# The first and the last pair of gate/up tiles in the FFN of a DiT step: a plain product ahead of the combined operands, and a read-back within the last pair

## The chip, the cores and the metric

The kernel runs on one core of one Trainium2 chip. Its time is the device time of one execution in microseconds (us); lower is better. The engines are called PE (TensorE, matmuls; PEld is its weight load), DVE (VectorE), ACT (ScalarE), POOL (GpSimd) and SP (SyncE, which issues nearly all DMAs here).

## The reference

One denoising step of a network with two layers, the first with differential attention, the second with a Hyena long convolution. Each is followed by a SwiGLU feed-forward network (FFN). The model's width is 1024, that of the FFN 2816. There are 1024 latent tokens and 128 context tokens, 1152 in all. Everything is float32. The part that the change touches is:

```python
def rmsnorm(x, g, eps=EPS):
    y = xf * lax.rsqrt(jnp.mean(xf * xf, axis=-1, keepdims=True) + eps)
    return (y * g.astype(jnp.float32)).astype(x.dtype)

def modulate(h, shift, scale):
    return h * (1.0 + scale) + shift

def swiglu(h, w_gu, w_down):
    g, u = jnp.split(h @ w_gu, 2, axis=-1)
    return (jax.nn.silu(g) * u) @ w_down
...
    for i in range(DEPTH):
        ...
        xs = xs + g1 * out
        h = modulate(rmsnorm(xs, norm2_g[i]), sh2, sc2)
        xs = xs + g2 * swiglu(h, ffn_w_gu[i], ffn_w_down[i])
```

Latent and context tokens have their own shift, scale and gate.

## The kernel before

Activations lie transposed: features on the 128 partitions, tokens along the free axis. `xk[k]` (k = 0 to 7) holds 128 features for all tokens as a left and a right half of 576 tokens. Each fp32 product is three products of parts: a number is split into a high part, copied by ACT (line 1550), and a low part, the difference, by DVE (line 1551), both in `part`; `three` (lines 305 to 307) adds high × high, high × low and low × high in PSUM.

The FFN of a layer (`ffn`) has three stages.

`project` multiplies by the output projection and adds the residual (line 857), in three chunks of 384 tokens. The norm of a chunk is `step(c)`: squares are summed over k on POOL (`nacc`, line 420), PE adds them over the partitions (430), a few tiny instructions on ACT and DVE make the reciprocal root (437 to 444), PE spreads it over the partitions (449), DVE multiplies (889) and ACT applies scale and shift (891). The left half's operands `b0` (k 0 to 3) and `b1` (k 4 to 7) are split in the same step; chunk 2 (tokens 768 to 1151) lies wholly in the right half.

`gate_up` goes through 22 tiles of the FFN's width. Tile t has a gate and an up part, which together form a pair: 2 × 2 blocks (gate and up; k 0 to 3 and k 4 to 7) times 2 × 2 blocks (k halves; left and right tokens). The kernel takes seven products in place of eight, after Winograd: p1, p2, p6, p7, p5, p4, p3, each 4 k × 2 column halves × 3 = 24 matmuls of 128x288, so 168 a pair. Their weight sides come from sums of the four weight blocks, made on POOL (`side_sums`), their token sides are b0, b1, b2 (right half, k 4 to 7) and t1 to t4, differences and sums of blocks of both halves that are formed once per layer by `combos`:

```python
        def second():
            for k in range(4):
                tt(u[:, k], b[k], f(low[0][0], k), SUB)
                tt(u[:, k], u[:, k], f(low[0][1], k), SUB)
                tt(v[:, k], b[k + 4], u[:, k], SUB)
                self.part(t2[0][:, k], t2[1][:, k], v[:, k])
```

`second` makes t2 for p6, `third` t3 for p7, `first` t1 for p5, `fourth` t4 for p4 (on POOL), `last` b2 for p3. The results, silu(gate) × up for each half, go to DRAM as `d_a[l][t]` (lines 1064 and 1072). A `pr` tile is a pair of PSUM banks, three of them in turn. Pairs 0 and 1 are interleaved: p1 and p2 of both come first, while the operands are formed.

`down` reads `d_a` back (line 1131) in groups of tiles, `GROUPS = [2, 4, 4, 4, 4, 4]`, splits them into `hs` tiles (six of them, three a group), multiplies with `mm` tiles of 128x384 in PSUM (six banks) and adds to x, which is loaded again by `load_x` (line 838, from `d_r`). It does so once per group. Weight tiles pass through `raw` (two buffers) to `wh` and `wl` (three each), by `fetch` (line 291).

Within `gate_up` the order on PE, DVE, ACT and POOL is the order in which the code is written (`pin`). A scheduler sets the order on SP, and everywhere else. Every engine works its instructions in order and waits on semaphores.

Of the kernel before, what the change touches and what calls it, by code (L numbers as in the profile page):

```python
# [150 lines left out]
class Net:  # L151
# [720 lines left out]
    def project(self, l, bx):  # L872
# [11 lines left out]

        def step(c):
            rs = self.rstd(c)
            for k in range(KT):
                for x, s, e, _ in self.whole(c, k):
                    nc.vector.tensor_tensor(out=x, in0=rs[:, s:e], in1=x, op=ALU.mult)
                for x, s, e, g in self.x(c, k):  # L890
                    nc.scalar.activation(x, x, AF.Identity, scale=a[:, k, g : g + 1], bias=sh[:, k, g : g + 1])  # L891
# [27 lines left out]

    def combos(self, low, bx, tp):  # L920
        nc, tt = self.nc, self.tt
        ADD, SUB = ALU.add, ALU.subtract
        t1, t2, t3 = (self.operand(tp, f"t{j}") for j in range(1, 4))
        top = self.operand(bx, "b2")
        u, v = (self.tl(tp, [P, 4, HALF], tag="t4" + n) for n in "hl")
        f = lambda t, k: t[:, k].bitcast(F32)
        b = [self.xk[k][1] for k in range(KT)]
        self.ops = ops = {1: low[0], 2: low[1], 3: top, 5: t1, 6: t2, 7: t3}

        def second():  # L930
            for k in range(4):
                tt(u[:, k], b[k], f(low[0][0], k), SUB)
                tt(u[:, k], u[:, k], f(low[0][1], k), SUB)
                tt(v[:, k], b[k + 4], u[:, k], SUB)
                self.part(t2[0][:, k], t2[1][:, k], v[:, k])

        def third():
            for k in range(4):
                tt(b[k], b[k + 4], b[k], SUB)
                self.part(t3[0][:, k], t3[1][:, k], b[k])  # L940

        def first():
            for k in range(4):
                self.part(t1[0][:, k], t1[1][:, k], u[:, k])

        def fourth():
            for k in range(4):
                tt(b[k], f(low[1][0], k), v[:, k], SUB, nc.gpsimd)
                tt(b[k], b[k], f(low[1][1], k), ADD, nc.gpsimd)
            t4 = ops[4] = self.operand(tp, "t4")  # L950
            for k in range(4):
                self.part(t4[0][:, k], t4[1][:, k], b[k])

        def last():
            for k in range(4):
                self.part(top[0][:, k], top[1][:, k], b[k + 4])

        return second, third, first, fourth, last
# [706 lines left out]
```

## Time and profile before

| | us |
|---|---|
| median of three runs | 3252.56 (3246.09 to 3252.89) |
| the profiled execution | 3253.19 |
| its span | 3251.4 |
| PE busy | 3081.2 (95%) |
| DVE busy | 1946.7 (60%) |
| ACT busy | 1183.5 (36%) |
| POOL busy | 1012.0 (31%) |

The mean granted clock of PE is 0.971 of full speed. In a row of instructions the first number is the start in us, the second the duration; "out<-in" are the program's tiles without their buffer numbers; "[1.44 <-DVE xk L857]" says that the engine was idle for 1.44 us just before, and what ended it. An engine's busy time counts overlapping matmuls once. In rows of groups stand count, busy time in us, mean of one in ns, and idle time ahead of them.

### The profile page before, as it was taken

What the parts mean: (1) busy time and instruction counts of PE and PEld (TensorE: products, weight loads), DVE (VectorE), ACT (ScalarE), POOL (GpSimd) and SP (SyncE); (2) the same over time, 40 slices, a digit from 0 to 9 for tenths busy, and PEclk for the clock granted to TensorE, in tenths of its full rate; (3) what the DMA queues carried; (4) which work ended last, traced back from release to release, by engine and by line L of the source; (5) the groups of instructions that cost most, each with busy time, mean ns of one, the idle gap of its engine ahead of it and who ended that gap; (6) DMA issues with size and microseconds to landing.
All of it is one profiled execution on the core that took longest, in us unless ns stands there. A gap on an engine that the chain in (4) does not pass through costs nothing.

```text
span 3251.4 us, 53225 instructions
## 1 busy us (share of the span) xinstructions
PE 3081.2 (95%) x21322; PEld 2988.6 (92%) x21322; DVE 1946.7 (60%) x3139; ACT 1183.5 (36%) x2284; POOL 1012.0 (31%) x866
## 2 busy tenths in 40 slices
PE   7899999999996999998999999999977999998998
PEld 5689989999995999998999999999976999998998
DVE  7866524988637544544544588875456544546555
ACT  3541224888634222222211442335543222222214
POOL 5844301444323434432000313131224434430003
PEclk9999999999996999999999999999987999999999
DMA  6665452444220222224563233345511222225221
GB/s 247 212 203 174 143 159 63 100 96 100 92 93 18 82 75 75 75 74 152 198 221 137 98 118 112 126 164 195 173 45 52 71 78 72 75 74 206 71 80 65
DMA packets 163343, 379.14 MB, mean 117 GB/s; under 512 B 17263, under 2 KB 80119, under 8 KB 160408
## 3 DMA queue, kind: packets, MB, share of 16 engines
q1 hardware_dynamic: 147720, 353.37, 33.0%
q10 hardware_dynamic: 13968, 17.65, 1.5%
q0 software_dynamic: 1408, 4.72, 0.4%
q8 instruction: 168, 2.75, 0.4%
q14 instruction: 79, 0.65, 0.1%
HBM read 278.94 MB, written 96.73 MB: 116 GB/s over the span
## 4 chain that ended last, share of the span: by engine, by line
PE 80%; DVE 6%; DMA 4%; ACT 2%; issue 2%; POOL 1%; SPq 0%; POOLq 0%; ACTq 0%; DVEq 0%
PE mm L305 13%; PE mm L306 13%; PE mm L307 12%; PE pr L306 10%; PE pr L307 10%; PE pr L305 10%; PE tr L785 4%; PE sc L759 2%; PE tr L776 2%; PE sc L760 2%; PE tr L368 1%; PE tr L307 1%; PE tr L305 1%; PE tr L306 1%; ACT xk L891 1%
## 5 line engine op out<-in xcount | busy, mean ns | idle before, releaser
L305 PE MATMUL mm<-hs,wh 128*128 128x384 f32 x1824 | 611.3, 338 | 17.5 <-ACT hs L1550 17.5
L306 PE MATMUL mm<-hs,wh 128*128 128x384 f32 x1824 | 614.2, 337 | 0.4 <-POOL hs L463 0.3
L307 PE MATMUL mm<-hs,wl 128*128 128x384 f32 x1824 | 612.5, 336 | 0.0
L857 DVE SCALAR_TENSOR_TENSOR xk<-mm,ada,xk 128x192 f32<-128x192 f32 (+3 forms) x560 | 233.3, 453 | 335.5 <-PE mm L307 329.8
L1165 DVE TENSOR_TENSOR xk<-pr,xk 128x576 f32<-128x576 f32 x220 | 166.0, 755 | 424.8 <-PE pr L307 228.2
L305 PEld LDWEIGHTS mm<-hs,wh 128*128 128x128 f32 x1824 | 343.5, 189 | 23.1 <-ACT hs L1550 18.0
L306 PEld LDWEIGHTS mm<-hs,wh 128*128 128x128 f32 x1824 | 344.2, 189 | 4.2 <-issue 1.8
L307 PEld LDWEIGHTS mm<-hs,wl 128*128 128x128 f32 x1824 | 344.0, 189 | 2.2 <-issue 0.8
L420 POOL TENSOR_TENSOR nacc<-nacc,nsq 128x384 f32<-128x384 f32 x104 | 119.2, 1146 | 703.1 <-ACT nsq L416 701.2
L1165 POOL TENSOR_TENSOR xk<-xk,xk 128x576 f32<-128x576 f32 x88 | 127.6, 1450 | 568.2 <-DVE xk L1165 454.1
L1550 ACT ACTIVATE wh<-raw 128x1024 fp32r<-128x1024 f32 x152 | 160.7, 1058 | 374.6 <-PE mm L306 330.0
L1551 DVE TENSOR_TENSOR wl<-xk,wh 128x512 fp32r<-128x512 f32 x176 | 196.1, 1153 | 71.3 <-ACT wh L1550 70.8
L1551 DVE TENSOR_TENSOR wl<-raw,wh 128x1024 fp32r<-128x1024 f32 x152 | 192.5, 1267 | 64.8 <-ACT wh L1550 64.4
L305 PE MATMUL mm<-hh,wh 128*128 128x384 f32 x576 | 193.5, 339 | 3.3 <-ACT hh L521 2.8
L306 PE MATMUL mm<-hl,wh 128*128 128x384 f32 x576 | 194.9, 338 | 0.7 <-DVE hl L522 0.7
L307 PE MATMUL mm<-hh,wl 128*128 128x384 f32 x576 | 194.7, 338 | 0.0
L766 DVE TENSOR_REDUCE nm<-sc 128x1 f32<-128x1152 f32 x128 | 173.6, 1357 | 35.1 <-PE sc L760 35.0
L1070 ACT ACTIVATE xk<-xk 128x576 f32<-128x576 f32 x44 | 30.2, 686 | 387.0 <-DVE xk L1165 387.0
L768 ACT ACTIVATE pr<-sc,nm 128x1152 f32<-128x1152 f32 x128 | 156.6, 1223 | 14.9 <-DVE nm L766 8.9
L759 PE MATMUL sc<-kk,qs 128*128 128x384 f32 x384 | 140.7, 366 | 3.3 <-ACT pr L768 3.3
L785 PE MATMUL tr<-v,at 128*128 128x128 f32 x1152 | 139.4, 275 | 0.5 <-ACT at L780 0.5
L785 PEld LDWEIGHTS tr<-v,at 128*128 128x128 f32 x1152 | 133.8, 192 | 3.1 <-ACT at L780 0.9
(367 smaller groups left out, 8543.6 us busy)
## 6 DMA issues: line engine op xcount, KB each, us to landing
raw<-w_gu SPq DMA_DIRECT2D x88, 512.0 KB, 3.4
araw<-ada_w SPq DMA_DIRECT2D x64, 512.0 KB, 4.5
d_a<-xk SPq DMA_DIRECT2D x88, 288.0 KB, 2.1
araw<-d_a SPq DMA_DIRECT2D x44, 576.0 KB, 7.9
raw<-w_down SPq DMA_DIRECT2D x44, 512.0 KB, 3.5
kk<-d_k SPq DMA_DIRECT2D x16, 1152.0 KB, 8.5
raw<-w_in SPq DMA_DIRECT2D x24, 512.0 KB, 3.5
hl<-ada_w SPq DMA_DIRECT2D x23, 512.0 KB, 6.9
```

Source lines behind the costliest of these rows:

```text
L305: self.nc.tensor.matmul(out, ah, bh, start=first, stop=False, **kw)
L306: self.nc.tensor.matmul(out, ah, bl, start=False, stop=False, **kw)
L307: self.nc.tensor.matmul(out, al, bh, start=False, stop=last, **kw)
L420: nc.gpsimd.tensor_tensor(out=self.acc[c], in0=self.acc[c], in1=sq, op=ALU.add)
L759: nc.tensor.matmul(sc[:, c, :CH], lhs, kk[:, 0, p, ks], start=True, stop=False)
L766: nc.vector.tensor_reduce(out=nm, in_=sv, axis=AX.XY, op=ALU.max, negate=True)
L768: nc.scalar.activation(e.rearrange("p (a b) -> p a b", a=3), sv, AF.Exp, bias=nm, accum_out=st[hd][3][:, p, qt : qt + 1])
L785: self.nc.tensor.matmul(po[:, :P], at[:, b], v[:, b], start=b == 0, stop=b == 8)
L857: self.nc.vector.scalar_tensor_tensor(out=x, in0=ps[:, s:e], scalar=gate[:, d, g : g + 1], in1=x, op0=ALU.mult, op1=ALU.add)
L1165: (eng or self.nc.vector).tensor_tensor(out=o, in0=a, in1=b, op=op)
L1550: self.nc.scalar.activation(hi, x, AF.Copy)
L1551: self.nc.vector.tensor_tensor(out=lo, in0=x, in1=hi.bitcast(F32), op=ALU.subtract)
```

## The change

**The first pair.** `rstd` becomes a generator, so that chunk 2's norm can be put between matmuls. Pair 0's gate and up are computed as eight plain products: first the left half in two column halves of 288, interleaved with chunk 2's norm and with p1 of pair 1, then the right half with its own split operands (`right`, in the memory of t4, and b2). The combined operands are then formed in the `xk` tiles themselves: with aa, bb the left and right half of k 0 to 3 and dd, ee those of k 4 to 7, bb −= aa (POOL), ee −= bb (DVE, gives t2), aa = ee − aa (DVE, t3), dd −= ee (POOL, t4 up to the signs that the products need), and t1 is bb. The low parts of the first three weight tiles and of some of pair 1's are made by POOL instead of DVE, as is the scale and shift of the context tokens. The rest of pair 1 follows alone, with its copies in halves.

**The last pair.** The first group of `down` has four tiles now. They are read back as eight half tiles into `xk` buffers during the last pair, split into the memory of b0 and b1, and used from there; two weight tiles of `down` and the 16 loads of x are also written into that pair. `GROUPS` is `[4, 4, 4, 4, 2, 4]`.

```diff
-GROUPS = [2, 4, 4, 4, 4, 4]
+GROUPS = [4, 4, 4, 4, 2, 4]
...
+        def apply(c, k, rs):
+            for x, s, e, _ in self.whole(c, k):
+                nc.vector.tensor_tensor(out=x, in0=rs[:, s:e], in1=x, op=ALU.mult)
+            for x, s, e, g in self.x(c, k):
+                if g:
+                    nc.gpsimd.tensor_scalar(
+                        out=x, in0=x, scalar1=a[:, k, g : g + 1], scalar2=sh[:, k, g : g + 1], op0=ALU.mult, op1=ALU.add
+                    )
+                else:
+                    nc.scalar.activation(x, x, AF.Identity, scale=a[:, k, g : g + 1], bias=sh[:, k, g : g + 1])
...
-        raws(0), sums(0), pair(0, 1), pair(0, 4), raws(1), pair(1, 1)
-        p1(0), p1(1)
-        pair(0, 2), second()
-        p2(0), p2(1)
-        pair(0, 3)
-        p6(0), third()
-        p7(0), first()
-        p5(0), fourth(), sums(1), pair(1, 2), pair(1, 4), raws(2)
-        p4(0), last()
-        p3(0), pair(1, 3)
...
+        g11, g12 = self.side_two(st[0]["raw"][0], eng=pool)
+        u21, u22 = self.side_two(st[0]["raw"][1], eng=pool)
+        raws(1)
+        pair(1, 1, pool)
+        norm = self.rstd_parts(NCH - 1)
...
+        for h in range(2):
+            self.times(gate, g11, ops[1], True, [h])
+            self.times(gate, g12, ops[2], False, [h])
+            if h == 0:
+                next(norm)
+            self.times(up, u21, ops[1], True, [h])
+            self.times(up, u22, ops[2], False, [h])
+            if h == 0:
+                rs = next(norm)
+            self.times(one["a"], one["w"][1], ops[1], True, [h])
...
+        for k in range(4):
+            apply(NCH - 1, k, rs)
+        for k in range(4):
+            self.part(*act(right, k), bb[k])
+            tt(bb[k], bb[k], aa[k], LESS, pool)
+            apply(NCH - 1, k + 4, rs)
+        close(0, gate, up)
+        copies(one, "s1", AF.Copy, "nacc", 3)
+        for k in range(4):
+            self.part(*act(ops[3], k), ee[k])
+        gate, up = bank(), bank()
+        self.times(gate, g11, right, True)
+        self.times(up, u21, right, True)
+        self.times(gate, g12, ops[3], False)
+        self.times(up, u22, ops[3], False)
+        for k in range(4):
+            tt(ee[k], ee[k], bb[k], LESS)
+            self.part(*act(t2, k), ee[k])
+        pair(1, 2)
+        for k in range(4):
+            tt(aa[k], ee[k], aa[k], LESS)
+            self.part(*act(t3, k), aa[k])
+        for k in range(4):
+            tt(dd[k], dd[k], ee[k], LESS, pool)
+        close(1, gate, up)
+        pair(1, 3, pool)
+        ops[6], ops[7] = t2, t3
+        p2(1, "nsq", 2)
+        p6(1)
...
+        t, stage = HT - 1, []
+        pair(t, 3)
+        p1(t)
+        for k in range(GROUPS[0]):
+            for h in range(2):
+                stage.append(self.tl(self.xp, [P, HALF], tag="xk", bufs=16))
+                nc.sync.dma_start(stage[-1], self.d_a[l][k][:, HALF * h : HALF * h + HALF])
...
+        p6(t), stretch(0)
+        p2(t)
+        p7(t), self.fetch()
+        p5(t), stretch(1)
+        self.load_x(self.d_r[l])
+        p4(t), self.fetch()
+        p3(t)
...
-    def part(self, hi, lo, x):
+    def part(self, hi, lo, x, eng=None):
         self.nc.scalar.activation(hi, x, AF.Copy)
-        self.nc.vector.tensor_tensor(out=lo, in0=x, in1=hi.bitcast(F32), op=ALU.subtract)
+        (eng or self.nc.vector).tensor_tensor(out=lo, in0=x, in1=hi.bitcast(F32), op=ALU.subtract)
```

`close(n, ...)` takes Silu of the gate (ACT), multiplies by up (DVE) and stores half n of pair 0. `stretch(j)` is four `part` of half tiles. `side_two` and `pair` split weight tiles into `wh` and `wl`.

What the change moves, at three places. First POOL, layer 0, at the end of the projection: chunk 1's last sum of squares and chunk 2's three (`nacc` 10086), then the sums of weights. Before:

```order
L420 TENSOR_TENSOR nacc_10076<-nacc_10076,nsq_10739 128x384
L420 TENSOR_TENSOR nacc_10086<-nacc_10086,nsq_10772 128x384
L420 TENSOR_TENSOR nacc_10086<-nacc_10086,nsq_10874 128x384
L420 TENSOR_TENSOR nacc_10086<-nacc_10086,nsq_10905 128x384
L1165 TENSOR_TENSOR xk_10978<-raw_10975 128x512
```

Now:

```order
L420 TENSOR_TENSOR nacc_10076<-nacc_10076,nsq_10739 128x384
L1637 TENSOR_TENSOR wl_10925<-raw_10920,wh_10924 128x1024
L420 TENSOR_TENSOR nacc_10086<-nacc_10086,nsq_10772 128x384
L1637 TENSOR_TENSOR wl_10929<-raw_10921,wh_10928 128x1024
L420 TENSOR_TENSOR nacc_10086<-nacc_10086,nsq_10874 128x384
L1637 TENSOR_TENSOR wl_10937<-raw_10932,wh_10936 128x1024
L420 TENSOR_TENSOR nacc_10086<-nacc_10086,nsq_10905 128x384
L1251 TENSOR_TENSOR t1h_10944<-raw_10933 128x512
```

Three low parts of weight tiles stand between chunk 2's sums.

Second ACT, at the forming of the operands. Before, t2's high parts directly follow the weights of p6, and t3's the weights of p5 and p3:

```order
L1550 ACTIVATE wh_11056<-xk_10979 128x512
L1550 ACTIVATE wh_11056<-xk_10980 128x512
L1550 ACTIVATE t2h_10966<-t4l_10973 128x576 x4
L1040 ACT_TABLE_LOAD
L1040 ACTIVATE xk_11106<-pr_11002 128x576
L1040 ACTIVATE xk_11132<-pr_11029 128x576
```

Now, from t2's last high part on (`t1l` holds pair 0's results, `nsq` the two halves of Silu of pair 1's gate, whose bank `pr_10942` p6 takes next):

```order
L1636 ACTIVATE t2h_11092<-xk_9940 128x576
L1636 ACTIVATE wh_11261<-t1h_10944 128x512 x2
L1636 ACTIVATE t3h_11094<-xk_9910 128x576
L1636 ACTIVATE t3h_11094<-xk_9914 128x576
L1636 ACTIVATE t3h_11094<-xk_9918 128x576
L1636 ACTIVATE t3h_11094<-xk_9922 128x576
L1096 ACTIVATE t1l_10943<-pr_11151 128x576
L1636 ACTIVATE wh_11286<-t1h_10944 128x512 x2
L1016 ACTIVATE nsq_11316<-pr_10942 128x288
L1016 ACTIVATE nsq_11317<-pr_10942 128x288
```

The copies that empty the bank for p6 stand behind all of t3 and the Silu of pair 0's second half.

Third SP, layer 0, in the last pair (`d_a_45_107` is pair 20's result, `d_a_46_108` pair 21's, `d_r` is x). Before:

```order
L1064 DMA d_a_45_107<-xk_15520 128x576
L1072 DMA d_a_45_107<-xk_15573 128x576
L291 DMA raw_15968<-w_down 128x1024
L838 DMA xk_15867<-d_r_9_71 128x576
...
L838 DMA xk_15889<-d_r_14_76 128x576
L1064 DMA d_a_46_108<-xk_15723 128x576
L838 DMA xk_15891<-d_r_15_77 128x576
L1131 DMA araw_2703_15905<-d_a_25_87 128x1152
```

Now:

```order
L1019 DMA d_a_45_107<-xk_15526 128x576
L1157 DMA xk_15704<-d_a_25_87 128x576
L1019 DMA d_a_45_107<-xk_15579 128x576
L1157 DMA xk_15706<-d_a_25_87 128x576
L1157 DMA xk_15708<-d_a_26_88 128x576
L1157 DMA xk_15710<-d_a_26_88 128x576
L1157 DMA xk_15712<-d_a_27_89 128x576
L1157 DMA xk_15714<-d_a_27_89 128x576
L1157 DMA xk_15716<-d_a_28_90 128x576
L1157 DMA xk_15718<-d_a_28_90 128x576
L844 DMA xk_15851<-d_r_9_71 128x576
```

The read-back of the first four tiles (`d_a_25_87` to `d_a_28_90`) goes out right behind pair 20's second store, ahead of x and of pair 21's stores.

More of the change, by code (lines that the diff above doesn't have):

```diff
@@ L914, in project @@
                         step(c - 1)
-        return low, step
+        return low, apply
     def operand(self, pool, tag):
         return tuple(self.tl(pool, [P, 4, HALF], F32R, tag=tag + n) for n in "hl")
[L920 to L958, printed above, removed]
     def side_load(self, l, t):
@@ L1068, in p3 @@
             mul(t, 3)
-            tt(q["s1"], q["b"], q["s1"], ALU.add)
-            nc.scalar.activation(q["s1"], q["s1"], AF.Silu)
-            tt(q["r"], q["s1"], q["r"], ALU.mult, nc.gpsimd)
-            nc.sync.dma_start(self.d_a[l][t][:, HALF:NT], q["r"].rearrange("p a b -> p (a b)"))
-            del st[t]
-        second, third, first, fourth, last = combos
-        raws(0), sums(0), pair(0, 1), pair(0, 4), raws(1), pair(1, 1)
-        p1(0), p1(1)
-        pair(0, 2), second()
-        p2(0), p2(1)
@@ L1080, in gate_up @@
[L1080 to L1089 removed]
+            for h, y in q["s1"]:
+                tt(y, q["b"][:, h], y, ADD)
+                nc.scalar.activation(y, y, AF.Silu)
+                tt(q["r"][:, h], y, q["r"][:, h], MUL, pool)
+            store(t, 1, q["r"])
@@ new lines, in p3, with flat @@
+            del st[t]
+        def flat(t, n):
+            return t[:, n].rearrange("p (a b) -> p a b", a=2)
+        raws(0)
+        g11, g12 = self.side_two(st[0]["raw"][0], eng=pool)
[3 more added lines that the diff above has]
+        norm = self.rstd_parts(NCH - 1)
+        gate, up, one = bank(), bank(), st[1]
+        one["a"] = bank()
+        kept, early = (self.tl(tp, [P, 4, HALF], tag=n) for n in ("t1l", "t1h"))
+        sums(1, [early[:, j, 0:512] for j in range(4)])
@@ new lines, in gate_up @@
+        for k in range(4):
[5 more added lines that the diff above has]
+        p6(1)
+        ops[5] = self.operand(tp, "t1")
+        for k in range(4):
+            self.part(*act(ops[5], k), bb[k])
+        p7(1)
+        pair(1, 4, pool)
+        raws(2)
+        ops[4] = self.operand(tp, "t4")
+        for k in range(4):
+            self.part(*act(ops[4], k), dd[k])
+        p5(1), sums(2), pair(2, 1)
@@ new lines, in gate_up, with stretch @@
+        p1(t)
+        for k in range(GROUPS[0]):
+            for h in range(2):
+                stage.append(self.tl(self.xp, [P, HALF], tag="xk", bufs=16))
+                nc.sync.dma_start(stage[-1], self.d_a[l][k][:, HALF * h : HALF * h + HALF])
+        views = []
+        def stretch(j):
+            view = [y.rearrange("p a b -> p (a b)") for y in self.operand(bx, f"b{j}")]
+            views.append(view)
+            for n in range(4):
+                c = slice(HALF * n, HALF * n + HALF)
+                self.part(view[0][:, c], view[1][:, c], stage[4 * j + n])
```

147 lines of the change are left out of this document (89 added, 58 removed).

## The prediction

> **What bounds the kernel now.** I read the page's busy shares and chain first, then stretches of the FFN by windows, then the timeline of single instructions.
>
> ```profile
> PE 3081.2 (95%) x21322; PEld 2988.6 (92%) x21322; DVE 1946.7 (60%) x3139; ACT 1183.5 (36%) x2284; POOL 1012.0 (31%) x866
> PE   7899999999996999998999999999977999998998
> PE 80%; DVE 6%; DMA 4%; ACT 2%; issue 2%; POOL 1%; SPq 0%; POOLq 0%; ACTq 0%; DVEq 0%
> ```
>
> TensorE (PE) bounds the kernel: 95% busy. What can be won stands in the few slices under 9, and two kinds of them lie in the FFN of each layer: its first pairs of tiles, and the passage to the down projection. Columns of the next view: stretch in us, its length, busy time and instructions of PE, PEld, DVE, ACT, POOL, then the granted clock.
>
> ```profile
> 980.00:1085.76 105.76, 70.89 (x357) 62.42 (x356) 74.08 (x107) 42.94 (x83) 40.44 (x25) 0.73 0.12 38
> 1085.76:1531.92 446.16, 446.16 (x3362) 445.93 (x3360) 216.45 (x218) 112.56 (x179) 176.72 (x116) 1.00 0.23 80
> 1531.92:1546.00 14.08, 5.28 (x17) 5.28 (x17) 6.38 (x15) 5.59 (x11) 1.86 (x1) 0.64 1.03 409
> 2398.90:2502.30 103.40, 66.78 (x345) 58.58 (x345) 73.53 (x104) 42.94 (x83) 39.66 (x25) 0.74 0.12 39
> ```
>
> The second row is 20 pairs without a pause at full clock: 446.16/20 = 22.31 us a pair, and 446.16/3360 = 0.1328 us a matmul. The first row holds the two pairs before them: 104.9 us from the projection's last broadcast (980.85 below) to the third pair, where two pairs need 44.6. So 60 us are lost there, partly to waits and partly to the clock of 0.73. The fourth row is the same stretch of layer 1 (103.4). The third row is the passage: 5.28 us busy of 14.
>
> ```profile
> 980.24 0.61 PE L449 MATMUL tr<-ndg,ones 128*128 128x128 f32 x4
> 982.29 0.37 PE L305 MATMUL pr<-b0h,wh 128*128 128x288 f32 x1 [1.44 <-DVE xk L857]
> 1085.76 0.30 PE L305 MATMUL pr<-b0h,wh 128*128 128x288 f32 x1
> 1531.63 0.29 PE L307 MATMUL pr<-b2h,wl 128*128 128x288 f32 x1
> 1540.72 1.97 PE L305 MATMUL mm<-hs,wh 128*128 128x384 f32 x5 [8.80 <-ACT hs L1550]
> 1544.41 0.53 PE L307 MATMUL mm<-hs,wl 128*128 128x384 f32 x1
> 1544.73 0.53 PE L306 MATMUL mm<-hs,wh 128*128 128x384 f32 x1
> 2957.26 1.01 PE L305 MATMUL mm<-hs,wh 128*128 128x384 f32 x2 [8.73 <-ACT hs L1550]
> ```
>
> These mark the ends: the first gate/up product, the third pair's first product, the last product of all pairs, and the first matmuls of the down projection, which wait 8.80 and 8.73 us for the read-back. Four us later they still start 0.32 apart; by columns full clock would give 0.1328 × 384/288 = 0.177. So I count the 5.28 busy us of the third window as half clock.
>
> **The start, before.** After the projection the vector engine works, not PE. For each of four k it forms t2 by three subtractions and a split, then t3 by one and a split:
>
> ```profile
> 1013.53 0.75 DVE L1165 TENSOR_TENSOR t4h<-xk,b0h 128x576 f32<-128x576 f32 x1
> 1015.11 0.76 DVE L1165 TENSOR_TENSOR t4l<-xk,t4h 128x576 f32<-128x576 f32 x1
> 1016.61 0.76 DVE L1551 TENSOR_TENSOR t2l<-t4l,t2h 128x576 fp32r<-128x576 f32 x1 [0.75 <-ACT t2h L1550]
> 1017.29 0.75 DVE L1165 TENSOR_TENSOR t4h<-xk,b0h 128x576 f32<-128x576 f32 x1
> 1029.03 0.75 DVE L1165 TENSOR_TENSOR xk<-xk,xk 128x576 f32<-128x576 f32 x1
> 1029.82 0.68 ACT L1550 ACTIVATE t3h<-xk 128x576 fp32r<-128x576 f32 x1 [2.17 <-DVE xk L1165]
> 1031.21 0.75 DVE L1165 TENSOR_TENSOR xk<-xk,xk 128x576 f32<-128x576 f32 x1
> 1031.37 1.86 POOL L1165 TENSOR_TENSOR xk<-b1h,t4l 128x576 f32<-128x576 f32 x1 [37.03 <-DVE t3l L1551]
> 1033.31 1.80 POOL L1165 TENSOR_TENSOR xk<-xk,b1l 128x576 f32<-128x576 f32 x1
> 1033.77 1.95 DVE L1165 TENSOR_TENSOR xk<-xk,xk 128x576 f32<-128x576 f32 x1
> ```
>
> A k of t2 takes 1017.29 − 1013.53 = 3.76 us, a k of t3 1031.21 − 1029.03 = 2.18. As soon as POOL works beside it the same DVE subtraction takes 1.95 instead of 0.75, and it ends (1035.72) about one free DVE duration after POOL's instruction does (1035.11): the two go one after the other. So I add POOL and DVE where both read SBUF.
>
> **The start, after.** The new path has the prices below (a line, its count, then its busy total and mean in ns); the last row is half-clock pace.
>
> ```profile
> L889 DVE TENSOR_TENSOR xk<-tr,xk 128x384 f32<-128x384 f32 x8 | 4.0, 543 | 0.0
> L891 ACT ACTIVATE xk<-xk,ada,A 128x256 f32<-128x256 f32 x8 | 4.7, 589 | 1.2 <-DVE xk L889 1.2
> L1165 POOL TENSOR_TENSOR xk<-xk,xk 128x576 f32<-128x576 f32 x18 | 25.7, 1430 | 117.6 <-DVE xk L1165 96.1 <-ACT xk L1070 21.6
> 989.27 1.28 POOL L1165 TENSOR_TENSOR xk<-xk,raw 128x512 f32<-128x512 f32 x1
> 983.18 1.00 POOL L420 TENSOR_TENSOR nacc<-nacc,nsq 128x384 f32<-128x384 f32 x1 [0.83 <-ACT nsq L416]
> 993.36 0.38 PE L449 MATMUL tr<-ndg,ones 128*128 128x128 f32 x2
> L1035 ACT ACTIVATE xk<-pr 128x576 f32<-128x576 f32 x2 | 1.3, 640 | 3.7 <-PE pr L307 3.7
> L1040 ACT ACT_TABLE_LOAD x1 | 1.3, 1283 | 0.0
> L1550 ACT ACTIVATE wh<-xk 128x512 fp32r<-128x512 f32 x10 | 5.9, 625 | 10.3 <-POOL xk L1165 7.9 <-PE pr L307 2.4
> 1030.00:1040.00 10.00, 6.34 (x18) 4.52 (x18) 7.45 (x6) 2.35 (x4) 8.47 (x5) 0.50 0.00 0
> 1034.31 0.45 PE L307 MATMUL pr<-t3h,wl 128*128 128x288 f32 x1
> 1034.55 0.45 PE L305 MATMUL pr<-t3h,wh 128*128 128x288 f32 x1
> ```
>
> PE begins where it did. Its left-half plain products need nothing of chunk 2 and fill time that was idle; the plain pair costs 24 matmuls more, 3.2 us, beside the chain below. The chain, in the order of the queues:
> 1. Chunk 2's broadcast ends at 993.74 in before. POOL now holds three 128x1024 splits, each ahead of one of chunk 2's sums of squares (1.00). No row shows such a split on POOL; two 128x512 rows make 2.56 each (bounds 2.4 and 3.2, where DVE disturbs), 7.7 in all. About 4.5 of it falls into POOL's idle time; I put 3.4 late: 997.1 (bounds 993.7, none late, and 1001.4, all of it).
> 2. ACT's four affines stand ahead of the first split of the right half: 0.54 + 4 × 0.59 + 0.67 + 0.76 = 4.3.
> 3. Three more k, each a scaling, a split and POOL's in-place subtraction in turn: 3 × (0.54 + 0.76 + 1.43) = 8.2.
> 4. Last affine 0.59, table load 1.28, Silu 0.65, copies 0.65: 3.2. DVE waits here for the Silu.
> 5. b2: 0.67 + 4 × 0.70 = 3.5.
> 6. t2: per k one DVE subtraction, a POOL subtraction that starts on its result and goes ahead of the split, the split: 4 × (0.75 + 1.43 + 0.76) = 11.8. ACT's half (0.68) lies beside POOL's.
> 7. Two 128x512 splits of weights: 1.3. Then t3, 4 × 2.18 = 8.7 with POOL idle.
> 8. ACT's Silu, two halves of weights and the copies that free p6's bank: 0.65 + 1.25 + 0.6, of which 0.8 beside the last split: 1.7.
>
> Sum: 997.1 + 4.3 + 8.2 + 3.2 + 3.5 + 11.8 + 1.3 + 8.7 + 1.7 = 1039.8 for the start of pair 1's p6. p6 itself needs only t2 (ready about 1029), but ACT's order puts t3 and the copies ahead, so PE, which does four plain half products and p2 (120 matmuls, 15.9) from the Silu at 1012 on, idles from 1028 some 11 us. After it five products, 120 × 0.1328 = 15.9, small waits 1.1 (t1 and t4 formed in step), and half clock at first. The window of 1030 to 1040 has a clock of 0.50 with PE 6 tenths busy; at the passage 5.28 us at half clock cost 2.6. I take 2.6 here too: 1059.4 instead of 1085.76, a gain of 26.4. In layer 1 the same 78.6 us stand against 103.4: 24.8.
>
> A rule weighed here: the Trainium skill, "SBUF — State Buffer" ("SBUF: two separate sides"), says that a DVE instruction with two SBUF inputs and one of GpSimd (POOL) exclude each other for a whole instruction. By it steps 3 and 6 add as I added them; the trace agrees (1.95 for 0.75). Without it these steps would be 7.3 us shorter. It speaks against moving so much to POOL.
>
> **The passage.** Now eight half tiles are read back in the last pair, on SP behind pair 20's second store: its products end at 1531.92 − 22.31 = 1509.6, plus an addition, a Silu and POOL's multiplication (0.75 + 0.65 + 1.43), so 1512.5. 8 × 288 KB at the 409 GB/s of the third window are 5.8 us: about 1518.5. On DVE and ACT four splits stand ahead of the addition that p4 waits for (p4 starts about 1525.3): 1518.5 + 4 × 0.7 + 0.8 = 1522, slack 3. The last four splits and two weight splits fit before 1531.9. The 16 loads of x go ahead of the last stores, and x for the first rows is there. PE then keeps its pace and its clock: gains 8.8 + 2.6 − 0.3 and 8.7 + 2.6 − 0.3, together 22.1 (bounds 0, if the loads come late, and 22.8).
>
> **The groups.** The two-tile group is now fifth.
>
> ```profile
> L857 DVE SCALAR_TENSOR_TENSOR xk<-mm,ada,xk 128x192 f32<-128x192 f32 (+3 forms) x560 | 233.3, 453 | 335.5 <-PE mm L307 329.8
> L1551 DVE TENSOR_TENSOR hs<-araw,hs 128x384 fp32r<-128x384 f32 x132 | 67.2, 552 | 26.5 <-ACT hs L1550 26.5
> L1551 DVE TENSOR_TENSOR wl<-raw,wh 128x1024 fp32r<-128x1024 f32 x152 | 192.5, 1267 | 64.8 <-ACT wh L1550 64.4
> ```
>
> In its 144 matmuls (× 0.177 = 25.5 us) DVE has 40 residual steps (233.3/560 each, 16.7), 12 splits (6.6) and two of weights (2.5): 25.8. Before, the first group had the same and nothing waited, but its buffers were empty; now the last group's come free only as the fifth begins. Between 0 and 5 a layer I take 1.5: the excess by the rows is 0.3, and 5 would be a whole tile's three read-back splits and their transfer in the open.
>
> Sum against the profiled execution (3253.2, 0.6 over the median): −26.4 − 24.8 − 22.1 + 3 = −70.3, so 3182.9; against the median 3182.
>
> **The rivals.**
> - Half clock to the end of the start. From 997.1 PE has 312 matmuls before the third pair; at 0.24 (the last two rows) 74.9 us: 1073, PE then being the bound with no wait to be idle in. Gains 12.8 and 11.2: 3253 − 24 − 22 + 3 = 3210. For it: the window at 0.50 with PE 6.3 tenths busy. Against: from the third pair on, work without a pause goes at 1.00, and the new start has five products in a row. The Trainium skill, "TensorE: Matmul & The Clock Gate" (Part 1), has a free-running window of 3.4 us whose activity sets the next one's clock. By it only the first product or two after the wait is slow; the half pace that still held 4 us after the passage's wait fits two such windows.
> - POOL barely disturbs and the clock holds: steps 3 and 6 shorter by 7.3, no 2.6: 1049.5, gains 36.3 and 34.7, no loss in the groups: 3160. Against it the 1.95 row.
> - The plain product buys nothing, since chunk 2's chain is as long in the new order (POOL's splits at 3.2 and all steps disturbed): start 1085, only the passage wins: 3253 − 22 + 3 = 3234. Against it: 3.76 + 2.18 us per k before, 2.9 + 2.2 now.
> - The read-back lands late, since x, weights and stage share the queues at 409 GB/s: half the passage lost, 3194; all of it, 3205.
> - Slower: the lock on SBUF stretches the chain. 26 DVE instructions with two SBUF inputs stand between 997 and 1040; at the disturbed 1.95 each they add 26 × 1.2 = 31 us a layer, 3245; from 1.35 each (35 a layer) the kernel is slower, at 1.5 it is 3261. Against it: POOL has only eight 1.43-us instructions there, which are in the sum already, and can't disturb 26.
>
> **How the numbers follow.** Forecast 0.58 (its own range 3170 to 3200), half clock 0.17, no lock 0.12, late read-back 0.05, start buys nothing 0.05, slower 0.03. The time is the forecast's, 3182. The range reaches to the undisturbed case and the half clock: 3158 to 3214. A measurement of this kernel tells about 0.2%, 6.5 us, from no change: faster 0.95, same 0.02, slower 0.03.
>
> **What would show it.** Third pair's first product near 1059 (1049 to 1073); PE idle some 11 us ahead of pair 1's p6, released by ACT's copies; POOL's eight subtractions near 1.43 with DVE instructions of about 2 us beside them; clock near 1.00 from p7 on. Down's first matmul within 0.5 us of the last product. Any wait over 2 us at the start of the last group would refute the group term. A clock of 0.50 after p6 or a stall at p4 of the last pair would make the prediction wrong.

## The result, and the profile after

The changed kernel takes 3174.32 us against 3252.7: a ratio of 0.976, 95% interval 0.9741 to 0.9779. The median is over four executions; one of them, 3363.59 us at a granted clock of 0.844, ran in a slower state and is in no comparison, the other three have 3170.83 to 3174.84. The forecast was 3182 (3158 to 3214). The profiled execution took 3174.84 us, its span is 3172.9.

The page's busy shares and chain after:

```profile
PE 3054.7 (96%) x21370; PEld 2977.7 (94%) x21370; DVE 1914.8 (60%) x3103; ACT 1175.3 (37%) x2264; POOL 1017.6 (32%) x886
PE   6899999999998899999999999999998999999998
PE 81%; DVE 6%; DMA 3%; ACT 2%; issue 2%; POOL 1%; SPq 0%; POOLq 0%; ACTq 0%; DVEq 0%
```

PE still bounds it, and its dips are shallower (the slices with 6 and 77 now have 88 and 8). The stretches that answer to those shown before (start and end, length, busy time and count of PE, PEld, DVE, ACT, POOL, clock):

```profile
980.00:1058.78 78.78, 60.48 (x385) 58.38 (x385) 58.31 (x95) 40.53 (x79) 39.90 (x32) 0.87 0.09 31
1058.78:1504.94 446.16, 446.16 (x3362) 445.93 (x3360) 223.25 (x229) 117.14 (x188) 178.31 (x119) 1.00 0.26 87
1504.94:1506.00 1.06, 0.12 (x1) 0.15 (x2) 0.82 (x2) 1.06 (x2) 0.18 (x1) 1.00 1.05 385
2355.70:2433.54 77.84, 60.04 (x378) 58.10 (x376) 55.87 (x91) 39.29 (x76) 39.06 (x32) 0.85 0.09 31
```

The 20 steady pairs are as they were. The start fell from 105.8 to 78.8 us, the clock in it rose from 0.73 to 0.87, and the passage to the down projection is 1 us. PE's rows, with every wait over 1 us in the start:

```profile
982.18 0.37 PE L305 MATMUL pr<-b0h,wh 128*128 128x288 f32 x1 [0.69 <-DVE xk L863]
987.69 0.40 PE L306 MATMUL pr<-b1l,wh 128*128 128x288 f32 x1 [1.96 <-DVE b1l L1637]
996.29 1.78 PE L455 MATMUL tr<-ndg,ones 128*128 128x128 f32 x6 [2.09 <-DVE ndg L454]
1012.92 0.40 PE L305 MATMUL pr<-t4h,wh 128*128 128x288 f32 x1 [4.40 <-ACT t1l L1096]
1038.07 0.61 PE L305 MATMUL pr<-t2h,wh 128*128 128x288 f32 x1 [7.46 <-ACT t1l L1096]
1058.78 0.30 PE L305 MATMUL pr<-b0h,wh 128*128 128x288 f32 x1
1505.88 0.41 PE L305 MATMUL mm<-b0h,wh 128*128 128x384 f32 x1 [0.94 <-DVE xk L1251]
2880.24 0.42 PE L305 MATMUL mm<-b0h,wh 128*128 128x384 f32 x1 [0.94 <-DVE xk L1251]
```

Four waits are left in the start: for the low part of b1, for chunk 2's broadcast, for Silu ahead of the right half, and 7.46 us ahead of pair 1's p6.

What moves ahead of the FFN differs by some us from one profile to the next (the first product starts at 987.40 with the copies early and the splits on DVE, and at 976.36 with Silu and weights early besides, though the code is the same up to there). So the comparisons below go by stretches from one row of PE to another, in us: from the first product of gate/up to p6 and to the third pair, the gap between the last product and the down projection (from start to start, less the 0.13 us that a product takes; it can hold small matmuls of the modulation), from there to layer 1's first product, and from layer 1's down projection to the end of the span. Each row is one profile; the three kernels with the same start (the change, start only, two-tile group second) differ by 0.4 us in layer 0 and by 2.9 in layer 1, so a difference in layer 1 alone says little.

| kernel | median | to p6 (layer 0) | to third pair, layers 0 / 1 | gap, layers 0 / 1 | to layer 1 | to the end |
|---|---|---|---|---|---|---|
| before | 3252.7 | | 103.5 / 104.5 | 8.96 / 8.89 | 857.6 | 294.1 |
| the change | 3174.3 | 55.9 | 76.6 / 77.8 | 1.11 / 1.10 | 849.8 | 292.7 |
| start only | 3174.9 | 55.6 | 76.3 / 76.0 | 2.66 / 2.64 | 853.6 | 293.3 |
| passage only | 3222.6 | | 101.6 / 105.8 | 0 / 0 | 850.7 | 292.3 |
| before, b2 in a pool of its own | 3230.4 | | 103.4 / 101.2 | 1.11 / 0 | 852.3 | 293.5 |
| splits on DVE | 3169.8 | 51.9 | 71.1 / 74.7 | 1.10 / 1.10 | 850.4 | 292.4 |
| copies early | 3158.1 | 49.5 | 71.6 / 71.9 | 0 / 0 | 851.0 | 292.3 |
| subtractions for t4 late | 3171.8 | 53.0 | 72.8 / 76.2 | 1.10 / 1.11 | 851.6 | 292.0 |
| copies and Silu early | 3159.3 | 49.7 | 70.6 / 71.8 | 0 / 0 | 850.8 | 292.3 |
| the same, subtractions late | 3167.5 | 49.7 | 75.0 / 75.9 | 0 / 0 | 850.3 | 292.0 |
| copies early, splits on DVE | 3155.3 | 45.8 | 66.7 / 68.8 | 0 / 0 | 851.4 | 292.3 |
| the same, Silu and weights early | 3159.6 | 45.7 | 70.1 / 72.0 | 0 / 0 | 851.3 | 292.0 |
| two-tile group second | 3175.6 (one run) | 56.0 | 76.7 / 78.9 | 1.10 / 1.11 | 852.9 | 293.0 |

From before to the change, by its rows: starts −26.9 and −26.6, gaps −7.85 and −7.79, between −7.8, end −1.5; with −0.1 ahead and some hundredths in the steady pairs −78.5, the difference of the spans.

### The profile page after: what moved, and what is told of

The parts are those of the page before. It is cut to its first block, busy times and chain, and to the rows that moved or that the text cites. A ratio compares the mean times of both kernels' runs of the same rounds, so it can differ in the third digit from the quotient of the medians.

```text
span 3172.9 us, 53324 instructions
## 1 busy us (share of the span) xinstructions
PE 3054.7 (96%) x21370; PEld 2977.7 (94%) x21370; DVE 1914.8 (60%) x3103; ACT 1175.3 (37%) x2264; POOL 1017.6 (32%) x886
## 4 chain that ended last, share of the span: by engine, by line
PE 81%; DVE 6%; DMA 3%; ACT 2%; issue 2%; POOL 1%; SPq 0%; POOLq 0%; ACTq 0%; DVEq 0%
PE mm L305 13%; PE mm L306 13%; PE mm L307 13%; PE pr L305 10%; PE pr L307 10%; PE pr L306 10%; PE tr L791 4%; PE sc L765 2%; PE sc L766 2%; PE tr L782 2%; PE tr L368 1%; DMA zt<-d_z 1%; ACT xk L900 1%; PE tr L307 1%; PE tr L305 1%
## 5 line engine op out<-in xcount | busy, mean ns | idle before, releaser
L306 PE MATMUL mm<-hs,wh 128*128 128x384 f32 x1632 | 548.3, 336 | 0.4 <-POOL hs L469 0.3
L307 PE MATMUL mm<-hs,wl 128*128 128x384 f32 x1632 | 546.6, 335 | 0.0
L305 PE MATMUL mm<-hs,wh 128*128 128x384 f32 x1632 | 545.9, 336 | 0.0
L1251 DVE TENSOR_TENSOR xk<-pr,xk 128x576 f32<-128x576 f32 x204 | 154.0, 755 | 392.7 <-PE pr L307 206.4
L1251 POOL TENSOR_TENSOR xk<-xk,xk 128x576 f32<-128x576 f32 x96 | 139.1, 1449 | 558.7 <-DVE xk L1251 454.1
L306 PEld LDWEIGHTS mm<-hs,wh 128*128 128x128 f32 x1632 | 306.4, 188 | 4.7 <-issue 2.2
L305 PEld LDWEIGHTS mm<-hs,wh 128*128 128x128 f32 x1632 | 306.1, 188 | 3.4 <-DVE xk L863 1.8
L307 PEld LDWEIGHTS mm<-hs,wl 128*128 128x128 f32 x1632 | 306.5, 188 | 2.1 <-issue 0.6
L1637 DVE TENSOR_TENSOR wl<-xk,wh 128x512 fp32r<-128x512 f32 x160 | 180.0, 1165 | 50.4 <-ACT wh L1636 50.4
L647 POOL TENSOR_TENSOR pr<-pr,al 128x384 f32<-128x384 f32 x64 | 53.6, 837 | 260.1 <-DVE al L643 256.7
```

Of the source, the lines that this page charges most:

```text
L305: self.nc.tensor.matmul(out, ah, bh, start=first, stop=False, **kw)
L306: self.nc.tensor.matmul(out, ah, bl, start=False, stop=False, **kw)
L307: self.nc.tensor.matmul(out, al, bh, start=False, stop=last, **kw)
L1251: (eng or self.nc.vector).tensor_tensor(out=o, in0=a, in1=b, op=op)
L1637: (eng or self.nc.vector).tensor_tensor(out=lo, in0=x, in1=hi.bitcast(F32), op=ALU.subtract)
```

## The experiments

### Which part brought it

The start alone: `GROUPS`, the last pair and the down projection of the kernel before, in the changed kernel.

```diff
-GROUPS = [4, 4, 4, 4, 2, 4]
+GROUPS = [2, 4, 4, 4, 4, 4]
-        for t in range(2, HT - 1):
+        for t in range(2, HT):
...
-        t, stage = HT - 1, []
```

> The start of the change alone: plain first pair and operands formed in place, with the last pair, the down projection and its groups as before. Theory A, each part is worth what its own stretch shows: between the two traces the stretch from the first gate/up product to the third pair is 26.9 us shorter in layer 0 and 26.6 in layer 1, so 3252.7 - 53.5 = 3199, and the down projection waits 8.7 to 8.8 us for the read-back as before. Theory B, part of the gain ascribed to the passage (or the 5 us that the changed kernel gained between the two FFNs) came from the earlier start: 3194 or less. If the starts are worth less alone: above 3203.

The passage alone: the last pair and the down projection of the change in the kernel before.

```diff
-GROUPS = [2, 4, 4, 4, 4, 4]
+GROUPS = [4, 4, 4, 4, 2, 4]
-        for t in range(1, HT):
+        for t in range(1, HT - 1):
...
+        t, stage = HT - 1, []
```

> The passage alone: read-back in the last pair, four-tile first group and two-tile fifth group, with the first pairs as before. Theory A: 7.86 and 7.79 us of wait and twice 2.6 us of half clock go, and what the changed kernel gained besides between the FFNs (about 4.5 us from the down projection's groups and after it) comes with the groups: 3252.7 - 20.9 - 3.5 = 3228. Theory B, the extra gain came from elsewhere: 3232. My prediction had the two-tile fifth group cost 1.5 a layer: then 3235.

Measured: 3174.85 for the start alone (ratio to before 0.9765, 0.9751 to 0.978), far under the 3199 of its theory A (theory B has 3194 or less), and 3222.56 for the passage alone (0.9908, 0.9893 to 0.9923), under all that was expected. They don't add: 77 and 29 us alone, 78 together. The start alone has the whole gain, though its two starts are 55.6 us shorter (27.2 and 28.5), no more. The reason is in its first row of the down projection, which reads the `hs` tiles as before, and yet hardly waits:

```profile
1501.17 0.41 PE L305 MATMUL mm<-hs,wh 128*128 128x384 f32 x1 [1.48 <-DVE xk L1219]
```

What the three kernels share is the place of b2, of which the prediction said nothing: the change opens a pool `bt` for it, where it had been in one pool with b0 and b1. So the kernel before was run with that alone:

```diff
+        tpb = bt.enter_context(self.pool("bt", side="right"))
...
-        self.gate_up(l, self.combos(low, bp, tpool))
+        self.gate_up(l, self.combos(low, tpb, tpool))
...
+        bt.close()
         bx.close()
```

> The kernel before, with one thing changed: the tile b2 lies in a pool of its own, as in the change, so that the memory of b0 and b1 is free for the read-back while p4 and p3 of the last pair still run, and SP's order has the first three read-back loads right behind pair 20's second store, ahead of x. Theory A, the place of b2 was what held the read-back: the gap before the down projection falls from 8.96 to the 2.66 us of the run with the start alone, the half clock after it nearly goes, 6.3 + 2 us a layer: 3252 - 17 = 3235. Rival, the gap fell there because the earlier start changed something else (clock, queues): gap 9, 3252.

Measured: 3230.35 us, 0.994 (0.9921 to 0.9958); by the profile's stretches the gaps fall to 1.11 and 0. SP's queue shows how. Before (start, time taken, line, transfer, count):

```profile
1512.67 0.33 SPq L1072 DMA_DIRECT2D d_a<-xk  x1
1521.47 0.33 SPq L291 DMA_DIRECT2D raw<-w_down  x1
1521.85 6.24 SPq L838 DMA_DIRECT2D xk<-d_r  x10
1531.15 0.32 SPq L1064 DMA_DIRECT2D d_a<-xk  x1
1532.24 1.81 SPq L1131 DMA_DIRECT2D araw<-d_a  x3
```

With b2 in its own pool (first the last read of b0 by PE):

```profile
1515.79 0.29 PE L307 MATMUL pr<-b0h,wl 128*128 128x288 f32 x1
1515.97 0.33 SPq L1072 DMA_DIRECT2D d_a<-xk  x1
1516.35 6.93 SPq L1133 DMA_DIRECT2D araw<-d_a  x3
1525.13 9.71 SPq L838 DMA_DIRECT2D xk<-d_r  x10
1536.16 0.45 PE L305 MATMUL mm<-hs,wh 128*128 128x384 f32 x1
```

The read-back goes out 0.4 us behind pair 20's second store instead of 19.6 us. Before, it goes out 0.3 us after the last product of all (1531.63 + 0.29), which reads b2; now 0.3 us after the last product that reads b0 (1515.79 + 0.29). That fits the reading that the loads land in memory of that pool, and that with b0's part released on its own the scheduler puts them ahead of x; no view shows the addresses. Theory A holds: the place of one tile was what held the passage. Its 22 us by the medians (20 by the ratio) and the 55.6 us of the two starts make up the 77 of the start alone. The code that reads back within the last pair is worth what is left between start alone and change: 1.55 us of gap a layer, and up to 3.8 us of the stretch to layer 1, most of which the order of the groups may have (last experiment); in the medians 0.5 us, which the runs can't tell from nothing. No run parts the plain first pair from the operands formed in place, so how the 55.6 us divide between them stays open.

### What holds p6: banks

```diff
         for k in range(4):
+            if k == 1:
+                p2(1, "nsq", 2)
             tt(aa[k], ee[k], aa[k], LESS)
...
-        p2(1, "nsq", 2)
         p6(1)
```

> The Silu copies of pair 1's gate, whose bank p6 takes, stand on ScalarE after the first of t3's four splits instead of behind all of them and the Silu of pair 0. Theory A, p6 waited for its bank alone (its operand t2 was there 9 us earlier): p6 starts near 1032 instead of 1038.07, p7 at once when t3 is there (1038 to 1039), the third pair at 1053 to 1055.5 instead of 1058.78, so 3 to 6 us a layer: 3163 to 3168. Rival, the vector engine's chain behind it (t1's splits, which wait for GpSimd's weight splits) sets the third pair anyway: p6 early, but p5 waits, third pair at 1058, 3173.

Measured: 3158.11 us (0.9713, 0.9699 to 0.9728), so 16 us under the changed kernel, more than expected.

```profile
1030.13 0.40 PE L305 MATMUL pr<-t2h,wh 128*128 128x288 f32 x1 [0.99 <-ACT nsq L1016]
1036.61 0.61 PE L305 MATMUL pr<-t3h,wh 128*128 128x288 f32 x1 [3.02 <-ACT t1l L1096]
```

p6 starts 6.4 us earlier, the third pair 5.1 and 6.0. The bank needs a correction: in the changed kernel p6 waited for `t1l`, which is the Silu of pair 0's second half (ACT, 1037.38 to 1038.01), and not for the copies (1038.95). So the bank that the text ahead of the prediction gives to p6 (`pr_10942`), and that step 8 has the copies empty, was not the one that p6 took. With the copies early it is p6 that the copies release and p7 that the Silu does. In both the operand was there long before: t2's last part ended at 1028.35 in the changed kernel. By the stretches the starts give 11.0 us and the gaps, now 0, 2.2, so 13.2 of the 14.0 between the spans (3158.9 here).

So the Silu was moved too:

```diff
                 p2(1, "nsq", 2)
+                nc.scalar.activation(flat(kept, 1), gate, AF.Silu)
...
-        close(1, gate, up)
+        tt(flat(kept, 1), up, flat(kept, 1), MUL)
+        store(0, 1, flat(kept, 1))
```

> As the run with the early copies, and the Silu of pair 0's second half also goes behind the first of t3's splits on ScalarE. It empties the bank that p7 takes. In the trace of the early copies PE waits 3.02 us for it ahead of p7. Theory A (banks, not operands, hold the products): p7 follows p6 at about 1033.5 on that trace's clock and then takes t3 k by k (1030.3, 1032.4, 1034.6, 1036.8); no wait long enough for half clock is left; third pair at +67 to +69 after the first product instead of +71.6: 3149 to 3153. Rival, t3 and t1 set the pace: p7 early but waiting inside, third pair unchanged at +71, 3158.

Measured: 3159.26 us, no better than without. p7's wait is gone, and p5 waits instead (2.15 <-ACT t1h), since t1's high parts go into memory from which POOL still splits weights (ACT idles 2.15 <-POOL wl). The third pair is 0.9 and 0.1 us earlier. The rival holds.

### The lock between DVE and POOL

The four subtractions for t4 on POOL, moved behind its weight splits:

```diff
-        for k in range(4):
-            tt(dd[k], dd[k], ee[k], LESS, pool)
         close(1, gate, up)
         pair(1, 3, pool)
+        for k in range(4):
+            tt(dd[k], dd[k], ee[k], LESS, pool)
```

> GpSimd's four in-place subtractions that prepare t4 stand behind its weight splits instead of beside t2. Theory A, they hold up t2's low parts (1.44 us instead of 0.76 each in the trace): t2 takes 2.18 us a k instead of 2.86, p6 starts at 1035.3 instead of 1038.07. At the third pair at most 2.7 us a layer earlier, 3169, if t4 is still in time; if the subtractions now stand beside t1's and t4's splits, these stretch and it comes out at 3172 to 3178. Rival, t2's low parts wait for ScalarE and not for GpSimd: t2 stays at 2.86 a k.

In the changed kernel, t2's low part beside POOL, and t3's alone:

```profile
1017.64 1.44 POOL L1251 TENSOR_TENSOR xk<-xk,xk 128x576 f32<-128x576 f32 x1 [5.92 <-DVE xk L1251]
1018.26 1.44 DVE L1637 TENSOR_TENSOR t2l<-xk,t2h 128x576 fp32r<-128x576 f32 x1 [0.75 <-ACT t2h L1636]
1030.98 0.76 DVE L1637 TENSOR_TENSOR t3l<-xk,t3h 128x576 fp32r<-128x576 f32 x1 [0.75 <-ACT t3h L1636]
```

With the subtractions late:

```profile
1019.63 0.76 DVE L1637 TENSOR_TENSOR t2l<-xk,t2h 128x576 fp32r<-128x576 f32 x1 [0.75 <-ACT t2h L1636]
1020.30 0.75 DVE L1251 TENSOR_TENSOR xk<-xk,xk 128x576 f32<-128x576 f32 x1
1042.39 6.42 DVE L1637 TENSOR_TENSOR t1l<-xk,t1h 128x576 fp32r<-128x576 f32 x4
```

Measured: 3171.78 us (0.9752, 0.9736 to 0.9768). t2's low part falls from 1.44 to 0.76 and a k of t2 from 2.86 to 2.17; POOL's subtraction, which ran until 1019.08, had held it for 0.68 us. p6 comes 2.9 us earlier, as theory A has it. The price appears where it was expected: t1's four low parts take 6.42 where they took 3.05. In layer 0 the third pair is 3.8 earlier, in layer 1 1.7; the medians don't part this run from the change. On top of the early copies, where p6 no longer hangs on t2, the same move only costs:

> As the run before it, with GpSimd's four subtractions for t4 behind its weight splits as well. Theory A (the lock on SBUF): t2 at 2.18 instead of 2.86 us a k, so t2 and t3 2.7 us earlier, but the subtractions then stand beside t1's splits, which stretch (6.42 for four instead of 2.8 to 3.1 in the earlier run): third pair between 2.7 us earlier and 1 us later than without the move: 3144 to 3155. Rival (no lock): no change at all in the duration of t2's low parts.

Measured: 3167.5 us. t2's low parts are at 0.76 here too, but p6 starts where it did (49.7), and the third pair 4.4 and 4.2 us later: t1's four low parts take 6.89. Between them PE pauses some 0.3 us at a time, and the clock stays low: 0.50 from about 1041 to 1051, where without the move it was 0.50 from 1040 to about 1043.5.

```profile
1046.00:1048.00 2.00, 1.92 (x8) 1.57 (x8) 2.00 (x4) 1.42 (x2) 2.00 (x2) 0.50 0.00 0
```

Outside the expected range: the price was right in kind and larger than the 1 us allowed, since nothing was won ahead of it, and the low clock adds to it.

The first weight splits back on DVE:

```diff
-        g11, g12 = self.side_two(st[0]["raw"][0], eng=pool)
-        u21, u22 = self.side_two(st[0]["raw"][1], eng=pool)
+        g11, g12 = self.side_two(st[0]["raw"][0])
+        u21, u22 = self.side_two(st[0]["raw"][1])
-        pair(1, 1, pool)
+        pair(1, 1)
```

> The change with the low parts of the first three weight tiles made by VectorE instead of GpSimd. Theory A, my step 1: GpSimd's three splits of 2.4 to 3.3 us delay chunk 2's sums by about 4 us, but the chain then waits for VectorE, which would have 3 x 1.25 us more ahead of chunk 2's broadcast: chunk 2's broadcast, 996.3 in the changed kernel or +14.1 after the first product, moves by less than 2 us either way, 3171 to 3178. Rival, the lock: without GpSimd beside it VectorE runs its own splits of b0 and b1 at 0.55 instead of up to 2, and the broadcast comes 4 us or more earlier: 3166.

Measured: 3169.78 us (0.9761, 0.9735 to 0.9787). Chunk 2's broadcast starts 9.9 us after the first product instead of 14.1:

```profile
983.60 0.37 PE L305 MATMUL pr<-b0h,wh 128*128 128x288 f32 x1 [1.65 <-DVE xk L863]
993.53 0.68 PE L455 MATMUL tr<-ndg,ones 128*128 128x128 f32 x4 [2.47 <-DVE ndg L454]
```

In the changed kernel the same place shows POOL's splits and DVE beside them:

```profile
973.77 2.40 POOL L1637 TENSOR_TENSOR wl<-raw,wh 128x1024 fp32r<-128x1024 f32 x1 [3.79 <-ACT wh L1636]
980.34 3.28 POOL L1637 TENSOR_TENSOR wl<-raw,wh 128x1024 fp32r<-128x1024 f32 x1 [1.17 <-ACT wh L1636]
984.56 2.66 POOL L1637 TENSOR_TENSOR wl<-raw,wh 128x1024 fp32r<-128x1024 f32 x1
983.63 4.01 DVE L1637 TENSOR_TENSOR b1l<-xk,b1h 128x384 fp32r<-128x384 f32 x2
988.56 0.83 PE L435 MATMUL tr<-ones,nacc 128*128 128x1 f32 x6 [0.33 <-POOL nacc L420]
```

PE's sum for chunk 2 (988.56) starts 6.4 us after the first product; with the splits on DVE it starts at 987.07, 3.5 after it. So the sums do queue behind POOL's splits, as my step 1 had it. But they did not hold the broadcast. The sum ends at 989.39, and ACT takes its root (`nr`) only at 994.42, behind chunk 1's scale and shift. ACT had waited 5.07 us for DVE's multiplications of chunk 1, and DVE came to these behind the two splits of 128x384 that took 4.01 us, where one alone takes 0.55. In the changed kernel, then with the splits on DVE:

```profile
987.56 4.31 DVE L893 TENSOR_TENSOR xk<-tr,xk 128x192 f32<-128x192 f32 x16
994.42 0.25 ACT L442 ACTIVATE nr<-tr,eps 128x3 f32<-128x3 f32 x1
986.60 4.33 DVE L893 TENSOR_TENSOR xk<-tr,xk 128x192 f32<-128x192 f32 x16
988.58 0.24 ACT L442 ACTIVATE nr<-tr,eps 128x3 f32<-128x3 f32 x1
```

Counted from the first product, the multiplications start at 3.0 instead of 5.4 us, and the root at 5.0 instead of 12.2: it now stands ahead of most of chunk 1's instructions on ACT, and DVE's queue is what the chain waits for behind it. So 2.4 of the 4.2 us are DVE's earlier start; the rest comes with the other order on ACT, and no run parts the two. The rival's number came, and theory A's fell: DVE makes the three splits itself and still reaches chunk 1's multiplications earlier. At the third pair 5.5 and 3.2 us are won.

### A version from both

> The early copies together with the first weight splits on VectorE. If the two gains are of different places (the bank of p6; GpSimd's splits ahead of chunk 2's norm) they add: third pair at +66 to +68.5 after the first product in layer 0 and near +69 in layer 1, 3158 - 4 to 8 = 3150 to 3154. If p2's end on TensorE holds p6 by then, the second gain is lost: 3157.

The two edits together add in layer 0 (5.1 and 5.5 alone, 9.9 together) and nearly in layer 1 (6.0 and 3.2, 9.0): 3155.28 us, 0.9712 (0.9694 to 0.973), the lowest median of all and 1 us above the range expected, against 0.976 (0.9741 to 0.9779) for the change. From the copies alone (0.9713) the runs can't tell it; the stretches can.

```profile
1033.20 0.40 PE L305 MATMUL pr<-t2h,wh 128*128 128x288 f32 x1 [0.80 <-ACT nsq L1016]
1039.31 0.61 PE L305 MATMUL pr<-t3h,wh 128*128 128x288 f32 x1 [2.64 <-ACT t1l L1096]
```

With the second Silu early and the weight splits for p5 and p3 between t3's (the subtractions for t4 are written ahead of t3, so POOL's order stays):

```diff
+            if k == 2:
+                pair(1, 3, pool)
             tt(aa[k], ee[k], aa[k], LESS)
```

> As the run before it, with pair 0's second Silu early too (the bank of p7) and the splits of p5's and p3's weights between t3's instead of after them; t1's splits waited for these (2.15 us ahead of p5). If that wait was real: third pair 2 to 3 us earlier again, 3145 to 3150. Rival, the lock: GpSimd's splits beside t3 stretch t3's low parts by what p5 gains, and it comes out as the run before it.

Measured: 3159.62 us (0.9727, 0.9713 to 0.9742); third pair 70.1 and 72.0 instead of 66.7 and 68.8. By the medians it can't be told from the run before it, as the rival has it; by the stretches it is 3.5 and 3.2 us slower. One subtraction of t3 is stretched to 1.85, and POOL, done earlier, starts the next pair's sums beside t4's splits. The longest wait is another: t1's low parts wait 1.50 us for the store of pair 0's second half, which lies in their memory, and PE 1.92 us for them. From then on PE goes at half clock to about 1038.2. Of the 3.6 us that layer 0 needs more from p6 to the third pair, about half stands as waits of PE and half as half pace.

```profile
1024.04 1.85 DVE L1255 TENSOR_TENSOR xk<-xk,xk 128x576 f32<-128x576 f32 x1
1032.73 3.10 DVE L1641 TENSOR_TENSOR t1l<-xk,t1h 128x576 fp32r<-128x576 f32 x4 [1.50 <-DMA d_a<-t1l]
1033.88 0.61 PE L306 MATMUL pr<-t1l,wh 128*128 128x288 f32 x1 [1.92 <-DVE t1l L1641]
1036.48 6.02 DVE L1641 TENSOR_TENSOR t4l<-xk,t4h 128x576 fp32r<-128x576 f32 x4
1036.80 1.56 POOL L1255 TENSOR_TENSOR xk<-raw 128x512 f32<-128x512 f32 x1 [3.59 <-DMA raw<-w_gu]
```

### The groups

```diff
-GROUPS = [4, 4, 4, 4, 2, 4]
+GROUPS = [4, 2, 4, 4, 4, 4]
```

> The change with the two-tile group second instead of fifth. My prediction had the fifth place cost 1.5 us a layer for the last group's buffers; the trace shows no wait there. If the place is worth nothing, the stretch from the down projection's first matmul to layer 1's first product stays at 850 and the last stretch at 292 to 293. If the earlier order of groups was the reason for the 3 to 5 us that the down projection gained between the FFNs, the stretch grows to 852 or more.

Measured: one run, 3175.58 us. The stretch to layer 1 is 852.9 instead of 849.8, the last one 293.0 instead of 292.7. All profiles with the fifth place have 849.8 to 851.6, so by this one profile the fifth place is a gain of 1 to 3 us, where I had charged a loss of 1.5 a layer.

## Why the prediction was right, and where it was not

The measured 3174 lies 8 us under the forecast, inside its own range (3170 to 3200). By the stretches the starts gave 53.5 us for 51.2, the waits of the passage 15.6 for 16.9, and all that follows 9.2, where I had 5.2 for the clock and a loss of 3 for the groups. So most of the 8 us lies in the group term.

**The chain of the start** came nearly row by row: 996.29 + 1.78 = 998.1 for the broadcast (997.1), p6 at 1038.07 (1039.8), third pair at 1058.78 (1059.4), gains of 26.9 and 26.6 (26.4 and 24.8). Step 6, POOL's turn ahead of the split, is confirmed by the move of the subtractions, to 0.7 us a k. Three things were off. Step 8 named the copies as what empties p6's bank; it was the Silu ahead of them, hence 1.7 us too late. PE idled 7.46 us ahead of p6 and not some 11, since its products from 1012.92 on lasted until 1030.6 and not 1028 (part of them at a clock of 0.50, from 1014 to 1016), and p6 came sooner. And layer 1's term took 78.6 us against a window that I began at 2398.9, while the first product before was at 2398.30, and 78.6 counts from an earlier row than the first product: like against like the stretches are 104.5 and 77.8. (The half-clock rival's 997.1 + 74.9 is 1072.0, not 1073.)

**Step 1** put the delay by POOL's splits at 3.4 us; taking them away gave 4.2. That the sizes are near is luck. The prediction had the sums queue on POOL, but chunk 2's sum stood ready 5.0 us before ACT took its root; what was late was chunk 1, behind DVE's own splits of b1, stretched from 0.55 to 2 us each.

**The clock.** I took 2.6 us. In the changed kernel p6 went at half clock, from 1038.07 to about 1044.2, where p7 begins (the window from 1044 to 1046 has 0.94):

```profile
1034.00:1036.00 2.00, 0.00 (x0) 0.00 (x0) 1.25 (x2) 0.68 (x1) 0.00 (x0) 0.50 0.00 0
1042.00:1044.00 2.00, 2.00 (x11) 2.00 (x10) 0.00 (x0) 2.00 (x5) 0.00 (x0) 0.50 0.00 0
1046.00:1048.00 2.00, 2.00 (x18) 2.00 (x17) 2.00 (x4) 1.33 (x2) 0.00 (x0) 1.00 0.69 221
```

Half of 6.2 us is 3.1. The half clock to the end of the start, my first rival, did not come: steady work brought the clock back, as the forecast had it. The Trainium skill, "TensorE: Matmul & The Clock Gate" (Part 1), has free-running windows of about 3.4 us. By that, as an estimate, the clock returns at the end of the first whole window of work, between 3.4 and 6.8 us after PE's first matmul. The 6.2 us agree. The run with copies and Silu early and subtractions late does not: there the clock returned only some 10.7 us after p5's first matmul (1040.29), with pauses of some 0.3 us in between. Whether such pauses keep a window from counting as work no run here shows.

**The passage** had the right size (8.5 and 8.4 a layer with the waits alone, 7.85 and 7.79 measured, and the clock) and the wrong cause. I credited the read-back within the last pair. The runs showed that b2's place in a pool with b0 and b1 had held the loads: one tile in another pool gives 22 of the 29 us that the whole passage gives by itself, so the right size is luck. The sign of 0.5 us to the first matmul was missed too: PE waits 0.94, for DVE's reading of a PSUM tile. My rival on late loads did not cover this; the order on SP shown ahead of the prediction showed the loads move, and did not tell why.

**The groups**: 3 us of loss charged, none came. No wait for `hs` tiles stands in the changed trace. Between the FFNs the kernel even gained 7.8 where the clock explains 2.6. Up to 2 of it are the small matmuls of the second layer's modulation (`ada_step`, line 368: PE is busy with them for 28.2 us before, 26.1 after; 28.0 in the start alone and 27.8 with b2 in its own pool, which have the old groups), and 2.2 are waits in the Hyena layer that differ between profiles. Why those matmuls take less in the new order of groups is open.

**The slower rival** and the undisturbed one fell by the same rows: POOL's eight subtractions took 1.40 to 1.44 each, and four of them held t2's low parts for 0.7 to 0.8 each (1.42 to 1.53 us, where I had looked for about 2), not for nothing and not 26 times.

## What to carry to other kernels

When a transfer that could go early goes late, look at whose memory it lands in before writing it elsewhere in the program: here the tile that lived longest belonged in a pool of its own. When an operand is ready and its product still waits, follow the wait to the PSUM bank, and move the instruction that empties it ahead on its engine. Work given to GpSimd was paid for twice in these runs where VectorE read two operands from SBUF beside it (t1's low parts 6.42 for 3.05 us): charge it to VectorE's path, and move it to where VectorE is idle. And when two results are late together, as the sums and chunk 1 were here, look at which of them the next instruction in the queue stands behind.
